# A hybrid S5 and dilated-attention block: the undilated group's values of all head pairs projected in one wide granule beside the scan and taken through DRAM, with attention gates in their place

## The chip, the cores and the metric

The kernel runs on one core of one Trainium2 chip. The metric is the time of one execution on the device in microseconds; several runs are taken and their median is compared. TensorE (PE) does matrix products and transposes into eight PSUM banks of 128 x 512 float32. VectorE (DVE), ScalarE (ACT) and GpSimd (POOL) work on tiles in SBUF and PSUM. SyncE (SP) issues most of the transfers between DRAM and SBUF. Each engine takes its instructions in the order of the program and waits at semaphores for the others.

## The reference

One decoder layer on 512 tokens of width 1024, with a state-space branch and an attention branch that share one projection. Reduced to what matters:

```python
h = rms_norm(x, norm_w)
proj = h @ w_in
u_s, z_s, q, k, v, z_a, r_s, r_a = split(proj)   # 1024, 1024, 1536, 1536, 1536, 512, 1024, 1024 columns
y_s = s5_branch(u_s, ...)                  # diagonal complex scan, GELU, GLU
y_s = (y_s * silu(z_s)) @ w_ssm_out
q, k = rope(rms_norm(q)), rope(rms_norm(k))
y_a = dilated_attention(q, k, v)           # 3 groups of 8 heads of 64; (window, dilation) (128, 1), (512, 4), (2048, 16)
y_a = (y_a * silu(z_a)) @ w_attn_out
m = sigmoid(r_s) * y_s + sigmoid(r_a) * y_a
out = x + m @ w_o
```

The values v of the first group (window 128, dilation 1: the undilated one) and the gates z_a of the attention branch are the two parts of `proj` that the change concerns. Each is 512 columns wide, that is four pairs of heads of 128 columns.

## The kernel before

All products are float32 in three passes: each operand is split in a high part and a rest, and hi·hi, hi·lo and lo·hi are added in PSUM (`mm3`, L133). The weights come from DRAM in pieces of 512 KB in the order of a list, `plan` (L138), two pieces ahead (`look`). For each piece SP issues the load of `w_raw`, ACT makes `w_hi` (L246) and DVE the rest, `w_lo` (L248). `w_raw` has two buffers, `w_hi` and `w_lo` three each.

There are two forms of projection. A unit (`cm_unit`, L251) takes 128 columns of weights as the stationary operand and leaves the result with columns on partitions and tokens along the free axis: 8 x 3 matmuls of 512 into one bank. A wide granule (`wide_granule`, L666) takes 512 columns of weights as the moving operand and leaves four tiles of 128 tokens x 512 columns in four banks: its weights come in four quarters (`kq`), and for each quarter it goes over the four token tiles (`r`) with 6 matmuls each, 96 in all. Both forms need the same matmuls for the same columns. Time in the program is counted in beats: 6 matmuls each, so that a unit has 4 beats and a granule 16.

PSUM tiles are dealt in turn by `ps_tile`:

```python
deal = {"p": [0, 1, 2], "g": [3, 4, 5, 6, 7]}
dealt[kind] += 1
... tag="b%d" % tags[dealt[kind] % len(tags)]
```

The projections use kind p; everything else uses kind g. While a granule runs beside the scan, p has the banks 0 to 3 and g the banks 4 to 7, and the same counter goes on. A tile that gets a bank has to wait for the reader of that bank's last tile.

The projections beside the scan go through the list `order` (L161): after the units of u come four units of attention gates (`za`), eight of state-space gates (`zs`), one unit of undilated values (`v0`), a granule with q, k and v of the first head pair (`v`), and eight units of merge gates (`rs`). Between their beats stand the scan's own steps, by a list of `events` (L944 to L959) with a beat each; DVE does the scan (L744 to L769) while PE projects. The gates go through `silu2` (L613): a tanh on ACT into `th` (L616) and a scalar_tensor_tensor on DVE that reads `th` and the PSUM tile (L617), into `sza` for `za` or into a tile `z` for `zs`, which SP writes to DRAM (`gd`, L627).

The undilated values leave their unit with columns on partitions, and the attention needs them with tokens on partitions, in blocks of 128 consecutive tokens (the tokens of the activations are ordered in four tiles, each with every fourth token). So `v0_unit` (L683) copies the unit's bank to SBUF in permuted order on ACT (`vt`, L686), and a later step `finish` turns it with four transposes on PE (`vtp`) and copies it to `V[:, 0]` on ACT (L692). This is done once beside the scan, for head pair 0, and once in each of the first three rounds of the attention stage, for the next head pair. There `scoring` (L1314) puts `finish` right behind the transposes of q and k (`qtp`, `turn`), which read `qraw`, a tile that DVE makes with the norm and the rope (`qk_norm`, L975 to L998). `skip_bank` (L1300) passes over one bank of kind g where no `finish` stands. All PE instructions are held in the order of the code (`follow`, L62); for the other engines the scheduler decides.

Of the kernel before, what the change touches and what calls it, by code (L numbers as in the profile page):

```python
# [11 lines left out]
F32 = mybir.dt.float32  # L12
# [8 lines left out]
P = 128  # L21
D = 1024
S = 512
KT = D // P
NB = S // P
# [8 lines left out]
NP = 4  # L34
NG = 3
U0, ZS0, Q0, K0, V0, ZA0, RS0, RA0 = 0, 1024, 2048, 3584, 5120, 6656, 7168, 8192
# [16 lines left out]
def tile_hybrid_block(ctx: ExitStack, tc: tile.TileContext, x, positions, norm_w, w_in, lam_re, lam_im,  # L53
# [3 lines left out]
    act, dve, pool, sp = nc.scalar, nc.vector, nc.gpsimd, nc.sync  # L57
# [25 lines left out]
    dram = ctx.enter_context(tc.tile_pool(name="dram", bufs=1, space=DRAM))  # L83
    psum = ctx.enter_context(tc.tile_pool(name="psum", bufs=1, space=PSUM))
    deal = {"p": [0, 1, 2], "g": [3, 4, 5, 6, 7]}
# [22 lines left out]
    def bank(name):  # L108
        return ps_tile("g", name)
# [4 lines left out]
    def t2k(name, dtype=F32):  # L114
        return tmp.tile([P, 512], dtype, name=name, tag="t2k")
# [22 lines left out]
    plan, loaded, look = [], [], 2  # L138
# [11 lines left out]
    def cm_spec(w, c0, kts=KT):  # L150
        return (section(w, 0, kts, (c0, P)), kts, P)

    def wide_spec(w, *cols):
        return [(section(w, 2 * h, 2 * h + 2, *cols), 2, 512) for h in range(4)]
# [3 lines left out]
    def head(base, g, hp):  # L158
        return (base + g * 512 + hp * P, P)

    order = [("za", c) for c in range(NP)] + [("zs", c) for c in range(KT)] + [("v0", 0), ("v", 0)]  # L161
    order += [("rs", c) for c in range(KT)]
    for kind, c in order:
        if kind == "v":
            plan += wide_spec(w_in, head(Q0, 2, 0), head(K0, 2, 0), head(V0, 1, 0), head(V0, 2, 0))
        else:
            plan.append(cm_spec(w_in, {"za": ZA0, "zs": ZS0, "rs": RS0, "ra": RA0, "v0": V0}[kind] + c * P))
    for c in range(KT):
        plan.append(cm_spec(w_glu, c * P))
    for c in range(KT):  # L170
# [1 line left out]
    for hp in range(NP):  # L172
        plan += wide_spec(w_in, head(Q0, 0, hp), head(K0, 0, hp), head(Q0, 1, hp), head(K0, 1, hp))
        if hp == 0:
            plan += [cm_spec(w_in, RA0 + c * P) for c in range(n_ra + 1)]
        else:
            plan += wide_spec(w_in, head(Q0, 2, hp), head(K0, 2, hp), head(V0, 1, hp), head(V0, 2, hp))
            plan.append(cm_spec(w_in, V0 + hp * P))
    for c in range(n_ra + 1, KT):
        plan.append(cm_spec(w_in, RA0 + c * P))  # L180
    for c in range(KT // 2):
# [69 lines left out]
    def cm_unit(rh, rl, kts=KT, ps=None, at=()):  # L251
        hi, lo = get_w()
        if ps is None:
            ps = pj_tile()
        for k in range(kts):
            if k % 2 == 0:
                call(at, k // 2)
            mm3(ps, hi[:, k], lo[:, k], rh[:, k], rl[:, k], k == 0, k == kts - 1)
        return ps


    ident = cst.tile([P, P], F32, name="ident")
# [12 lines left out]
    hT_hi = cst.tile([P, KT, S], F32R, name="hT_hi")  # L275
    hT_lo = cst.tile([P, KT, S], F32R, name="hT_lo")
# [172 lines left out]
    W0, K0B, V0B, Y0 = 16, 49, 74, 88  # L449
# [169 lines left out]
    def za_unit(c, at=()):  # L619
        ps = cm_unit(hT_hi, hT_lo, at=at)  # L620
        silu2(sza[:, c], ps)
# [44 lines left out]
    def wide_granule(th, tl, at=(), halved=False):  # L666

        pss = [pj_tile() for _ in range(NB)] + ([bank("pj")] if halved else [])
        for kq in range(4):
            hi, lo = get_w()  # L670
            for r in range(NB):
                call(at, 4 * kq + r)
                parts = [(pss[r], slice(0, 512))]
                if halved and r == NB - 1:
                    parts = [(pss[r], slice(0, 256)), (pss[NB], slice(256, 512))]
                for ps, c in parts:
                    for k in range(2):
                        kk = 2 * kq + k
                        mm3(ps[:, c], th[:, kk, r * P:(r + 1) * P], tl[:, kk, r * P:(r + 1) * P], hi[:, k, c], lo[:, k, c],
                            kk == 0, kk == KT - 1)  # L680
        return pss

    def v0_unit(hp, V, at=()):  # L683
        ps = cm_unit(hT_hi, hT_lo, at=at)
        vt = t2k("vt")
        act.copy(vt.rearrange("p (b r j) -> p r b j", r=4, b=4), ps.rearrange("p (r b j) -> p r b j", r=4, b=4))  # L686

        def finish():
            pt = bank("vtp")
            for b in range(NB):  # L690
                pe.transpose(pt[:, b * P:(b + 1) * P], vt[:, b * P:(b + 1) * P], ident)
            act.copy(V[:, 0].rearrange("p b c -> p (b c)"), pt)  # L692
        return finish

    qd = dram.tile([2, P, 512], F32, name="qd")

    def qv_granule(V, at=()):
        few = dict(deal)
        deal.update(p=[0, 1, 2, 3], g=[4, 5, 6, 7])
        pss = wide_granule(hT_hi, hT_lo, at)  # L700
        deal.update(few)
        for b in range(2):
            qs = t2k("qs")
            for i in range(2):
                r = 2 * b + i
                act.copy(qs[:, 256 * i:256 * i + 256], pss[r][:, 0:256])
                act.copy(V[:, 1:3, r], pss[r][:, 256:512].rearrange("p (g c) -> p g c", g=2))
            sp.dma_start(qd[b], qs)
# [70 lines left out]
    scan_work += [lambda i=i: step(Xs[:, :, :, i], Xs[:, :, :, i - 1], Xs[:, :, :, i]) for i in range(1, NI)]  # L779

    V = new_v()
    fin = []

    def filler(kind, c, at):
        if kind == "v0":
            fin.append(v0_unit(0, V, at))
        elif kind == "v":
            qv_granule(V, at)
        else:
            {"u": u_unit, "za": za_unit, "zs": zs_unit, "rs": rs_unit}[kind](c, at=at)  # L790
# [103 lines left out]
    def load_us(j):  # L894
        Us[j] = load_u(j, uss[:, 512 * (j % 2):512 * (j % 2) + 512])
# [48 lines left out]
    events = [(3, begin_x), (6, lambda: early.update({3: load_u(3, sza[:, 3])})), (5, f_turn)]  # L944
# [9 lines left out]
    events += [(Y0 + (11 * j + 1) // 3 + 2, lambda j=j: turn_next(j)) for j in range(1, 4)]  # L954
    events += [(W0 + 16, tables_last)]
    events += [(W0 + 26 + 4 * i, lambda i=i: scanning(i, 11)) for i in range(11)]
    events += [(V0B, lambda: fin.pop()()), (Y0 - 10, lambda: load_us(0)), (Y0 - 10, lambda: load_us(1))]
    events += [(Y0 + (11 * j + 1) // 3, lambda j=j: chunk(j)) for j in range(8)] + [(Y0 + 28, lambda: gelu(7, y_turn(7), *gTs))]
    events = sorted(enumerate(events), key=lambda e: (e[1][0], e[0]))  # L959
    events = [e for _, e in events]  # L960
    b0 = 0
    for kind, c in [("u", j) for j in range(3, 8)] + order:
        n = 16 if kind == "v" else 4
        filler(kind, c, [(b - b0, f) for b, f in events if b0 <= b < b0 + n])
        b0 += n
    for b, f in events:
# [58 lines left out]
    def qk_first(at=()):  # L1025

        pss = wide_granule(hT_hi, hT_lo, at)
        raws = [new_raw(0), new_raw(1)]
        sq = sml.tile([P, NB, 8], F32, name="ssq")
        for r in range(NB):  # L1030
            for i in range(2):
                act.copy(raws[i][:, r], pss[r][:, 256 * i:256 * i + 256])
            squares(sq[:, r], pss[r])
        qk_norm((0, 1), raws, sq)
        return raws
# [271 lines left out]
    def turn(hp, g, a):  # L1307
        return lambda: qk_turn(g, (raws[0], raws[1], raw)[g], *QK, turned=(a,))
# [2 lines left out]
        ra_unit(c)  # L1311
    ra_unit(n_ra, [(3, turn(0, 0, 0)), (3, turn(0, 0, 1))])

    def scoring(hp, n, fin):  # L1314
        return [(n, turn(hp, 2, 0)), (n, turn(hp, 2, 1)), (n, fin),
                (n + 3, lambda: dilated(hp, (0, 1), *QK)), (n + 4, lambda: dilated(hp, (2, 3), *QK)),
                (n + 7, lambda: local(hp, *QK)), (n + 7, lambda: settle(hp))]

    def scoring_first(n):
        return [(0, turn(0, 1, 0)), (0, turn(0, 1, 1)), (n, lambda: local(0, *QK)), (n + 2, turn(0, 2, 0)),  # L1320
                (n + 2, turn(0, 2, 1)), (n + 2, skip_bank), (n + 6, lambda: dilated(0, (0, 1), *QK)),
                (n + 7, lambda: dilated(0, (2, 3), *QK)), (n + 7, lambda: settle(0))]

    def turning(hp, n):
        return [(n + i, lambda kind=kind, bb=bb: p_turn(hp, kind, bb))
                for i, (kind, bb) in enumerate(((0, 0), (0, 1), (1, 0), (1, 1)))]

    rals = {}
    fin = skip_bank
    for hp in range(NP):  # L1330
        if hp < NP - 1:
            raws = qk_first(scoring(hp, 3, fin) if hp else scoring_first(4))
            n = 3
            at = turning(hp, n) + [(n + 5, lambda hp=hp: values(hp))]
            at += [(n + 5 + 2 * g + a + (g + a > 0), turn(hp + 1, g, a)) for g in range(2) for a in range(2)]
            raw, Vs[hp + 1] = qk_second(at)
            fin = v0_unit(hp + 1, Vs[hp + 1])
        else:
            for c in range(2):
                rals[c] = gate_tile()  # L1340
                sp.dma_start(rals[c], rad[c])
            at = scoring(hp, 3, fin) + turning(hp, 16)
            for i, c in enumerate(range(n_ra + 1, KT)):
                ra_unit(c, [(n - 4 * i, f) for n, f in at if 4 * i <= n < 4 * i + 4])
            values(hp)
# [64 lines left out]
```

## Time and profile before

| | us |
|---|---|
| median of 3 runs | 672.55 |
| lowest, highest run | 670.82, 672.61 |
| the profiled execution, as timed | 670.11 |
| its span in the trace | 668.0 |
| granted TensorE clock | 1.00 |
| PE busy | 662.0 |
| DVE busy | 464.0 |
| ACT busy | 323.4 |
| POOL busy | 118.1 |

The profiled execution is one of its own, 2.4 us below the median of the runs. Its span goes from the first to the last instruction in the trace, 2.1 us less than its time. Durations in the trace are of single instructions; those on PE overlap with the next one, so the spacing of starts tells what a matmul costs.

### The profile page before, as it was taken

The numbers are of one execution on the slowest core, as the hardware profiler recorded it, in microseconds if no ns is written. First come the engines' busy times: TensorE is split into PE (matmuls) and PEld (weight loads), VectorE is DVE, ScalarE is ACT, GpSimd is POOL, SyncE is SP. The second block draws the span as 40 slices with busy tenths as digits, with TensorE's granted clock in tenths as the row PEclk, the third lists the DMA queues.
The fourth block names the chain that finished last, engine by engine and source line by source line (L and its number), as shares of the span: only waits on it lengthen the run. The fifth ranks groups of instructions, "written<-read, shape, count | busy, mean of one in ns | idle before, by whom it ended". The sixth has DMA issues, their size and how long they took to land.

```text
span 668.0 us, 12363 instructions
## 1 busy us (share of the span) xinstructions
PE 662.0 (99%) x4633; PEld 556.3 (83%) x4633; DVE 464.0 (69%) x965; ACT 323.4 (48%) x680; POOL 118.1 (18%) x274
## 2 busy tenths in 40 slices
PE   8999999999999999999999999999999999999997
PEld 8988888888888888888888888888888888888886
DVE  7999989999786476743238676758575956657531
ACT  6645454422677563422444574557356645633210
POOL 1110000600465258700000030012001200210000
PEclk9999999999999999999999999999999999999999
DMA  9656434743666653563244323222232313347231
GB/s 308 130 137 179 121 95 133 180 142 95 178 141 155 155 169 112 165 216 107 64 126 143 96 64 97 71 74 77 64 94 64 96 35 95 103 147 269 94 127 63
DMA packets 137954, 83.15 MB, mean 124 GB/s; under 512 B 32800, under 2 KB 125992, under 8 KB 137768
## 3 DMA queue, kind: packets, MB, share of 16 engines
q1 hardware_dynamic: 135544, 79.36, 40.2%
q0 software_dynamic: 2048, 2.36, 2.5%
q8 instruction: 36, 0.59, 0.4%
q10 hardware_dynamic: 304, 0.66, 0.3%
q14 instruction: 22, 0.18, 0.1%
HBM read 68.99 MB, written 11.01 MB: 120 GB/s over the span
## 4 chain that ended last, share of the span: by engine, by line
PE 96%; DVE 2%; DMA 1%; ACT 0%; issue 0%; ACTq 0%
PE pj L69 81%; PE sps L69 3%; PE yps L69 3%; PE ot L69 2%; PE ptp L74 2%; PE qtp L74 2%; PE xps L69 1%; PE wps L74 1%; DMA x_all<-in_x_dram 1%; PE kps L69 1%; PE yT L74 1%; DVE w_lo L248 0%; ACT w_hi L246 0%; DVE hT_lo L351 0%; PE vtp L74 0%
## 5 line engine op out<-in xcount | busy, mean ns | idle before, releaser
L246 ACT ACTIVATE w_hi<-w_raw 128x1024 fp32r<-128x1024 f32 x94 | 99.4, 1059 | 164.8 <-PE pj L69 124.8
L248 DVE TENSOR_TENSOR w_lo<-w_raw,w_hi 128x1024 fp32r<-128x1024 f32 x94 | 119.0, 1268 | 62.9 <-ACT w_hi L246 60.7
L69 PE MATMUL pj<-hT_hi,w_hi 128*128 128x512 f32 (+1 forms) x344 | 131.4, 384 | 0.0
L69 PE MATMUL pj<-hT_lo,w_hi 128*128 128x512 f32 (+1 forms) x344 | 128.8, 376 | 0.4 <-DVE hT_lo L351 0.4
L69 PE MATMUL pj<-hT_hi,w_lo 128*128 128x512 f32 (+1 forms) x344 | 126.8, 375 | 0.0
L69 PE MATMUL pj<-w_hi,hT_hi 128*128 128x512 f32 x256 | 102.7, 401 | 0.0
L69 PE MATMUL pj<-w_hi,hT_lo 128*128 128x512 f32 x256 | 99.9, 390 | 0.0
L69 PE MATMUL pj<-w_lo,hT_hi 128*128 128x512 f32 x256 | 99.9, 390 | 0.0
L69 PEld LDWEIGHTS pj<-hT_hi,w_hi 128*128 128x128 f32 x344 | 65.1, 189 | 11.0
L69 PEld LDWEIGHTS pj<-hT_lo,w_hi 128*128 128x128 f32 x344 | 64.9, 189 | 11.1 <-DVE hT_lo L351 0.6
L69 PEld LDWEIGHTS pj<-hT_hi,w_lo 128*128 128x128 f32 x344 | 63.7, 188 | 11.9
L69 PEld LDWEIGHTS pj<-w_hi,hT_lo 128*128 128x128 f32 x256 | 48.1, 188 | 10.4
L69 PEld LDWEIGHTS pj<-w_hi,hT_hi 128*128 128x128 f32 x256 | 48.1, 188 | 9.2
L69 PEld LDWEIGHTS pj<-w_lo,hT_hi 128*128 128x128 f32 x256 | 48.2, 188 | 8.7
L1114 POOL COPY sw<-st 32x4 f32<-32x4 f32 x64 | 11.8, 185 | 172.9 <-ACT Pt L1070 170.1
L1015 DVE SCALAR_TENSOR_TENSOR qkp<-qtp,wcol,qkp 128x512 fp32r<-128x512 f32 (+1 forms) x32 | 23.5, 748 | 25.3 <-ACT qkp L1014 25.2
L1070 ACT ACTIVATE Pt<-Pt,st 128x256 f32<-128x256 f32 (+1 forms) x64 | 30.9, 484 | 19.9 <-DVE st L1068 19.9
L1014 ACT ACTIVATE qkp<-qtp,wcol 128x512 fp32r<-128x512 f32 (+1 forms) x32 | 21.2, 683 | 34.3 <-PE qtp L74 30.9
L840 POOL DMA_DIRECT2D dd<-kt x64 | 33.7, 535 | 2.4 <-POOL kt L836 2.1
L69 PE MATMUL pj<-w_lo,mT_hi 128*128 128x512 f32 (+1 forms) x72 | 26.3, 366 | 0.0
L69 PE MATMUL pj<-w_hi,mT_hi 128*128 128x512 f32 (+1 forms) x72 | 26.3, 366 | 0.0
L69 PE MATMUL pj<-w_hi,mT_lo 128*128 128x512 f32 (+1 forms) x72 | 26.3, 365 | 0.0
(301 smaller groups left out, 1179.8 us busy)
## 6 DMA issues: line engine op xcount, KB each, us to landing
w_raw<-in_w_in_dram SPq DMA_DIRECT2D x36, 512.0 KB
w_raw<-in_w_in_dram SPq DMA_DIRECT2D x128, 128.0 KB
w_raw<-in_w_glu_dram SPq DMA_DIRECT2D x8, 512.0 KB
w_raw<-in_w_ssm_out_dram SPq DMA_DIRECT2D x8, 512.0 KB
w_raw<-in_w_o_dram SPq DMA_DIRECT2D x8, 512.0 KB
w_early<-in_w_in_dram SPq DMA_DIRECT2D x4, 512.0 KB
ud<-uT SPq DMA_DIRECT2D x8, 256.0 KB
uss<-ud SPq DMA_DIRECT2D x8, 256.0 KB
```

The costliest lines, as they stand in the source:

```text
L69: last[0] = nc.tensor.matmul(*a, **k)
L74: last[0] = nc.tensor.transpose(*a, **k)
L246: last_act[0] = act.activation(hi, raw, AF.Copy).ins
L248: dve.tensor_tensor(lo, raw, hi.bitcast(F32), op=ALU.subtract)
L840: pool.dma_start(M[Q * t:Q * t + Q, :, 0:P - Q * t], kt[:, :, t:].rearrange("q g k p -> q g (k p)"))
L1014: act.activation(hi, ps[sl], AF.Copy, scale=w)
L1015: dve.scalar_tensor_tensor(lo, ps[sl], w, hi.bitcast(F32), op0=ALU.mult, op1=ALU.subtract)
L1070: act.activation(o, o, AF.Exp, bias=nm, scale=-1.0, accum_out=st[:, kind, 1, h, b:b + 1])
L1114: pool.tensor_copy(sw[32 * r:32 * r + 32, :, :, b], st[32 * b:32 * b + 32, 1, :, :, r])
```

## The change

`order` has one unit of `za` instead of four, and in place of the unit `v0` a wide granule over the 512 columns of undilated values of all four head pairs. Each of its four token tiles is copied by ACT to an SBUF tile and written by SP to DRAM (`vd`). For each head pair `v0_load` reads its 128 columns back in four transfers, in the order of tokens that the attention needs; for pair 0 ten beats after `V0B`, for the others behind the projection of the round before. In the attention stage each `v0_unit` becomes a `za_unit`, and `skip_bank` takes the place of `finish`. The transposes `vtp` and their copies are gone. Banks for the new granule are set as for the old one, by the same lines, now a function `beside_scan`.

```diff
--- before.py
+++ after.py
@@ -158,13 +158,15 @@
     def head(base, g, hp):
         return (base + g * 512 + hp * P, P)
 
-    order = [("za", c) for c in range(NP)] + [("zs", c) for c in range(KT)] + [("v0", 0), ("v", 0)]
+    order = [("za", 0)] + [("zs", c) for c in range(KT)] + [("v0", 0), ("v", 0)]
     order += [("rs", c) for c in range(KT)]
     for kind, c in order:
-        if kind == "v":
+        if kind == "v0":
+            plan += wide_spec(w_in, (V0, 512))
+        elif kind == "v":
             plan += wide_spec(w_in, head(Q0, 2, 0), head(K0, 2, 0), head(V0, 1, 0), head(V0, 2, 0))
         else:
-            plan.append(cm_spec(w_in, {"za": ZA0, "zs": ZS0, "rs": RS0, "ra": RA0, "v0": V0}[kind] + c * P))
+            plan.append(cm_spec(w_in, {"za": ZA0, "zs": ZS0, "rs": RS0}[kind] + c * P))
     for c in range(KT):
         plan.append(cm_spec(w_glu, c * P))
     for c in range(KT):
@@ -175,7 +177,7 @@
             plan += [cm_spec(w_in, RA0 + c * P) for c in range(n_ra + 1)]
         else:
             plan += wide_spec(w_in, head(Q0, 2, hp), head(K0, 2, hp), head(V0, 1, hp), head(V0, 2, hp))
-            plan.append(cm_spec(w_in, V0 + hp * P))
+            plan.append(cm_spec(w_in, ZA0 + hp * P))
     for c in range(n_ra + 1, KT):
         plan.append(cm_spec(w_in, RA0 + c * P))
     for c in range(KT // 2):
@@ -680,25 +682,30 @@
                             kk == 0, kk == KT - 1)
         return pss
 
-    def v0_unit(hp, V, at=()):
-        ps = cm_unit(hT_hi, hT_lo, at=at)
-        vt = t2k("vt")
-        act.copy(vt.rearrange("p (b r j) -> p r b j", r=4, b=4), ps.rearrange("p (r b j) -> p r b j", r=4, b=4))
-
-        def finish():
-            pt = bank("vtp")
-            for b in range(NB):
-                pe.transpose(pt[:, b * P:(b + 1) * P], vt[:, b * P:(b + 1) * P], ident)
-            act.copy(V[:, 0].rearrange("p b c -> p (b c)"), pt)
-        return finish
-
-    qd = dram.tile([2, P, 512], F32, name="qd")
-
-    def qv_granule(V, at=()):
+    vd = dram.tile([NB, P, 512], F32, name="vd")
+
+    def beside_scan(at):
         few = dict(deal)
         deal.update(p=[0, 1, 2, 3], g=[4, 5, 6, 7])
         pss = wide_granule(hT_hi, hT_lo, at)
         deal.update(few)
+        return pss
+
+    def v0_granule(at=()):
+        pss = beside_scan(at)
+        for r in range(NB):
+            vt = t2k("vt")
+            act.copy(vt, pss[r])
+            sp.dma_start(vd[r], vt)
+
+    def v0_load(hp, V):
+        for r in range(NB):
+            sp.dma_start(V[32 * r:32 * r + 32, 0], vd[r, :, hp * P:hp * P + P].rearrange("(b j) c -> j b c", b=NB))
+
+    qd = dram.tile([2, P, 512], F32, name="qd")
+
+    def qv_granule(V, at=()):
+        pss = beside_scan(at)
         for b in range(2):
             qs = t2k("qs")
             for i in range(2):
@@ -779,11 +786,10 @@
     scan_work += [lambda i=i: step(Xs[:, :, :, i], Xs[:, :, :, i - 1], Xs[:, :, :, i]) for i in range(1, NI)]
 
     V = new_v()
-    fin = []
 
     def filler(kind, c, at):
         if kind == "v0":
-            fin.append(v0_unit(0, V, at))
+            v0_granule(at)
         elif kind == "v":
             qv_granule(V, at)
         else:
@@ -954,13 +960,13 @@
     events += [(Y0 + (11 * j + 1) // 3 + 2, lambda j=j: turn_next(j)) for j in range(1, 4)]
     events += [(W0 + 16, tables_last)]
     events += [(W0 + 26 + 4 * i, lambda i=i: scanning(i, 11)) for i in range(11)]
-    events += [(V0B, lambda: fin.pop()()), (Y0 - 10, lambda: load_us(0)), (Y0 - 10, lambda: load_us(1))]
+    events += [(V0B + 10, lambda: v0_load(0, V)), (Y0 - 10, lambda: load_us(0)), (Y0 - 10, lambda: load_us(1))]
     events += [(Y0 + (11 * j + 1) // 3, lambda j=j: chunk(j)) for j in range(8)] + [(Y0 + 28, lambda: gelu(7, y_turn(7), *gTs))]
     events = sorted(enumerate(events), key=lambda e: (e[1][0], e[0]))
     events = [e for _, e in events]
     b0 = 0
     for kind, c in [("u", j) for j in range(3, 8)] + order:
-        n = 16 if kind == "v" else 4
+        n = 16 if kind in ("v0", "v") else 4
         filler(kind, c, [(b - b0, f) for b, f in events if b0 <= b < b0 + n])
         b0 += n
     for b, f in events:
@@ -1311,8 +1317,8 @@
         ra_unit(c)
     ra_unit(n_ra, [(3, turn(0, 0, 0)), (3, turn(0, 0, 1))])
 
-    def scoring(hp, n, fin):
-        return [(n, turn(hp, 2, 0)), (n, turn(hp, 2, 1)), (n, fin),
+    def scoring(hp, n):
+        return [(n, turn(hp, 2, 0)), (n, turn(hp, 2, 1)), (n, skip_bank),
                 (n + 3, lambda: dilated(hp, (0, 1), *QK)), (n + 4, lambda: dilated(hp, (2, 3), *QK)),
                 (n + 7, lambda: local(hp, *QK)), (n + 7, lambda: settle(hp))]
 
@@ -1326,20 +1332,20 @@
                 for i, (kind, bb) in enumerate(((0, 0), (0, 1), (1, 0), (1, 1)))]
 
     rals = {}
-    fin = skip_bank
     for hp in range(NP):
         if hp < NP - 1:
-            raws = qk_first(scoring(hp, 3, fin) if hp else scoring_first(4))
+            raws = qk_first(scoring(hp, 3) if hp else scoring_first(4))
             n = 3
             at = turning(hp, n) + [(n + 5, lambda hp=hp: values(hp))]
             at += [(n + 5 + 2 * g + a + (g + a > 0), turn(hp + 1, g, a)) for g in range(2) for a in range(2)]
             raw, Vs[hp + 1] = qk_second(at)
-            fin = v0_unit(hp + 1, Vs[hp + 1])
+            v0_load(hp + 1, Vs[hp + 1])
+            za_unit(hp + 1)
         else:
             for c in range(2):
                 rals[c] = gate_tile()
                 sp.dma_start(rals[c], rad[c])
-            at = scoring(hp, 3, fin) + turning(hp, 16)
+            at = scoring(hp, 3) + turning(hp, 16)
             for i, c in enumerate(range(n_ra + 1, KT)):
                 ra_unit(c, [(n - 4 * i, f) for n, f in at if 4 * i <= n < 4 * i + 4])
             values(hp)
```

What this does to the order of instructions is shown at three places, with the names' numbers telling tiles apart. Line numbers are those of each kernel; the changed one is 2 lines further on around L617, 7 in the scan's steps and 6 in the attention stage.

The first place is on PE, beside the scan, at the end of the fourteenth unit of the loop over `order` and the units of u: before, the next is another unit (its `DVE_49` is the reader of a bank three units back). "waits" names the semaphore that the instruction waits for.

```order
L69 MATMUL pj_1526<-hT_hi_87,w_lo_1354 128x512
L69 MATMUL pj_1526<-hT_hi_87,w_hi_1353 128x512
L69 MATMUL pj_1526<-hT_lo_88,w_hi_1353 128x512
L69 MATMUL pj_1526<-hT_hi_87,w_lo_1354 128x512
L69 MATMUL pj_1568<-hT_hi_87,w_hi_1395 128x512 [waits DVE_49]
L69 MATMUL pj_1568<-hT_lo_88,w_hi_1395 128x512
L69 MATMUL pj_1568<-hT_hi_87,w_lo_1396 128x512
L69 MATMUL pj_1568<-hT_hi_87,w_hi_1395 128x512
```

After the change the fourteenth unit is the last of `zs`, and the next instruction is the first of the new granule:

```order
L69 MATMUL pj_1533<-hT_hi_87,w_lo_1361 128x512
L69 MATMUL pj_1533<-hT_hi_87,w_hi_1360 128x512
L69 MATMUL pj_1533<-hT_lo_88,w_hi_1360 128x512
L69 MATMUL pj_1533<-hT_hi_87,w_lo_1361 128x512
L69 MATMUL pj_1569<-w_hi_1402,hT_hi_87 128x512 [waits DVE_49]
L69 MATMUL pj_1569<-w_lo_1403,hT_hi_87 128x512
L69 MATMUL pj_1569<-w_hi_1402,hT_lo_88 128x512
L69 MATMUL pj_1569<-w_hi_1402,hT_hi_87 128x512
```

The tile `pj_1569` is the eighteenth of kind p and is dealt from four banks, `pj_1533` the seventeenth and dealt from three; both get bank 2. The wait on `DVE_49` is now for the reader of `pj_1533`.

The second place is on DVE at the same place of the program, first before the change:

```order
L749 TENSOR_TENSOR scn_522<-scn_522 128x512
L744 TENSOR_TENSOR scn_522<-scn_522 128x1024
L748 TENSOR_TENSOR scn_522<-Xs_548,scn_522 128x512
L248 TENSOR_TENSOR w_lo_1565<-w_raw_1562,w_hi_1564 128x1024
L749 TENSOR_TENSOR scn_522<-scn_522 128x512
L769 MEMSET Xs_548 128x64
L617 SCALAR_TENSOR_TENSOR z_1557<-th_1558,pj_1526 128x512
```

The same rows after the change, where the last one reads the bank that the granule waits for:

```order
L756 TENSOR_TENSOR scn_523<-scn_523 128x512
L751 TENSOR_TENSOR scn_523<-scn_523 128x1024
L755 TENSOR_TENSOR scn_523<-Xs_549,scn_523 128x512
L250 TENSOR_TENSOR w_lo_1576<-w_raw_1573,w_hi_1575 128x1024
L756 TENSOR_TENSOR scn_523<-scn_523 128x512
L776 MEMSET Xs_549 128x64
L619 SCALAR_TENSOR_TENSOR z_1564<-th_1565,pj_1533 128x512
```

Nothing moved here but names and line numbers: the reader of the unit's bank, the last row, stands behind two scan steps, a split of weights and a clearing of `Xs`.

The third place is on DVE in the attention stage, where the first of the three units changes its kind; before:

```order
L987 TENSOR_TENSOR qraw_4651<-qraw_4651,qrstd_4675 128x1024
L248 TENSOR_TENSOR w_lo_4743<-w_raw_4737,w_hi_4742 128x1024
L993 TENSOR_TENSOR rt1_4691<-qraw_4651,tC_3040 128x256
L994 TENSOR_TENSOR rt2_4692<-qraw_4651,tS_3041 128x16x8
L996 TENSOR_TENSOR rt2_4692<-qraw_4651,tS_3041 128x16x8
L998 TENSOR_TENSOR qraw_4651<-rt1_4691,rt2_4692 128x16x16
L1015 SCALAR_TENSOR_TENSOR qkp_3683<-qtp_4764,wcol_84,qkp_3682 128x512
```

After the change:

```order
L250 TENSOR_TENSOR w_lo_4748<-w_raw_4742,w_hi_4747 128x1024
L999 TENSOR_TENSOR rt1_4691<-qraw_4651,tC_3040 128x256
L1000 TENSOR_TENSOR rt2_4692<-qraw_4651,tS_3041 128x16x8
L1002 TENSOR_TENSOR rt2_4692<-qraw_4651,tS_3041 128x16x8
L619 SCALAR_TENSOR_TENSOR sza_337<-th_4735,pj_4710 128x512
L1004 TENSOR_TENSOR qraw_4651<-rt1_4691,rt2_4692 128x16x16
L1021 SCALAR_TENSOR_TENSOR qkp_3683<-qtp_4769,wcol_84,qkp_3682 128x512
```

The new row of `sza` stands between the three products of the rope and their sum, `qraw`.

## The prediction, on record before the run

> **What bounds the kernel now.** I begin with the share of each engine and the chain of work that ended last, since together they say whose time a saving has to come out of.
>
> ```profile
> span 668.0 us, 12363 instructions
> ...
> PE 662.0 (99%) x4633; PEld 556.3 (83%) x4633; DVE 464.0 (69%) x965; ACT 323.4 (48%) x680; POOL 118.1 (18%) x274
> ...
> PE 96%; DVE 2%; DMA 1%; ACT 0%; issue 0%; ACTq 0%
> ```
>
> TensorE is busy for 99% of the span and is 96% of the chain. So a matmul or transpose that goes shortens the span by its own time, and every new moment in which PE waits lengthens it by that moment. Work on other engines counts only where PE waits for it. VectorE is 69% busy on average, but the change acts beside the scan, so I read that stage by itself: the windows view (PE, PEld, DVE, ACT, POOL busy, clock, DMA share, GB/s).
>
> ```profile
> 120.00:130.00 10.00, 10.00 (x45) 8.26 (x44) 9.83 (x15) 3.09 (x4) 8.45 (x16) 1.00 0.74 152
> 140.00:150.00 10.00, 10.00 (x46) 8.24 (x45) 9.83 (x14) 3.08 (x4) 0.00 (x0) 1.00 0.51 158
> ```
>
> VectorE is at 9.83 of 10 us there: whatever is put into its queue comes out late. PE has no gap, because each projection unit fills a PSUM bank that was emptied long before. Which unit waits for which eviction is the question of this change.
>
> **What is removed.** Sixteen transposes on PE, and eight copies of 128x512 on ACT; the projection matmuls stay as many (one wide granule of 96 in place of four units of 24). The groups view (busy us and mean ns of one), then the chain at one place beside the scan and at one in the attention stage (start, us):
>
> ```profile
> L74 PE MATMUL vtp<-ident,vt 128*128 128x128 f32 x16 | 2.4, 272 | 0.0
> L692 ACT COPY V<-vtp 128x512 f32<-128x512 f32 x4 | 2.3, 574 | 1.9 <-PE vtp L74 1.9
> L686 ACT COPY vt<-pj 128x512 f32<-128x512 f32 x4 | 2.3, 563 | 0.0
> L616 ACT ACTIVATE th<-pj 128x512 f32<-128x512 f32 x12 | 6.9, 578 | 0.0
> ```
>
> ```profile
> 150.11 0.44 PE vtp L74 x4
> ```
>
> ```profile
> 435.25 0.44 PE vtp L74 x4
> ...
> 439.49 0.77 DVE qkp L1015
> 440.26 0.04 issue
> 440.30 1.21 PE sps L69 x8
> ```
>
> Each group of four takes 0.44 us of the chain, and there are four groups (one for each pair of heads): **-1.8 us**. The 2.4 us of the group's busy time count overlapping matmuls twice, so the chain's number is used. The ACT copies (four granule copies of 0.56 replace the four unit copies; the four of V, 0.57 each, go; tanh stays at twelve) are worth nothing either way: ACT is at 3.1 of 10 us. The stall before sps at 440.30 stays, as its chain starts when PE ends the first quarter of a granule, which moves with PE.
>
> **The wait that is added.** Banks for projections are dealt in turn: three while units run, four while a granule runs. In the order of dealing, the new granule's first tile is number 18, and 18 mod 4 = 2; the unit just before it is number 17, and 17 mod 3 = 2. It is **the same bank**. So the granule's first matmul has to wait until that last unit's silu has been read out: tanh on ACT and then a scalar_tensor_tensor on DVE (the order's rows show PE's wait on DVE there, and the DVE row that releases it reads pj_1533, the unit just ended). Before, a unit waited for the reader of the unit three earlier, and the old granule's first bank had a whole unit in between. All that PE has queued is behind this matmul, since its matmuls go in program order.
>
> How late that DVE instruction is can be read at the same place of the program before: fourteen units after the start of this loop, where the order has the same instructions on ACT and DVE up to it. The timeline, PE first, then ACT, then DVE:
>
> ```profile
> 125.02 0.39 PE L69 MATMUL pj<-hT_lo,w_hi 128*128 128x512 f32 x1
> 125.24 0.39 PE L69 MATMUL pj<-hT_hi,w_lo 128*128 128x512 f32 x1
> 125.47 0.39 PE L69 MATMUL pj<-hT_hi,w_hi 128*128 128x512 f32 x1
> ```
>
> ```profile
> 125.44 1.07 ACT L246 ACTIVATE w_hi<-w_raw 128x1024 fp32r<-128x1024 f32 x1 [3.90 <-PE pj L69]
> 126.41 0.58 ACT L616 ACTIVATE th<-pj 128x512 f32<-128x512 f32 x1
> ```
>
> ```profile
> 126.04 0.69 DVE L748 TENSOR_TENSOR scn<-Xs,scn 128x512 f32<-128x512 f32 x1
> 126.65 1.22 DVE L248 TENSOR_TENSOR w_lo<-w_raw,w_hi 128x1024 fp32r<-128x1024 f32 x1
> 127.79 0.68 DVE L749 TENSOR_TENSOR scn<-scn 128x512 f32<-128x512 f32 x1
> 128.46 0.65 DVE L617 SCALAR_TENSOR_TENSOR z<-th,pj 128x512 f32<-128x512 f32 x1
> ```
>
> The unit's last matmul starts at 125.24 and the next unit's first at 125.47. ACT first makes the high part of the next weights (w_hi), then the tanh, until 126.99. DVE has a scan step, the weights' low part and another step ahead of the silu, which runs from 128.46 to 129.11. With 0.04 us from DVE's end to PE's start, as before sps above, PE would begin at 129.15 and not at 125.47: **+3.7 us**. Bounds: if DVE took the silu the moment the tanh ended, 126.99 + 0.65 + 0.04 = 127.68, or +2.2 us. If DVE were as late as it was for an earlier gate,
>
> ```profile
> 78.65 0.58 ACT L616 ACTIVATE th<-pj 128x512 f32<-128x512 f32 x1
> ...
> 82.32 0.68 DVE L617 SCALAR_TENSOR_TENSOR sza<-th,pj 128x512 f32<-128x512 f32 x1
> ```
>
> which ended 3.77 us after its tanh (83.00 - 79.23), it would be 130.80, or +5.3. I take 3.7, the row at the same place. Nothing later gives it back: PE has no other wait for DVE in this stage that an earlier DVE would shorten. The granule's other banks were read before, or a unit earlier; its own banks are freed by ACT 0.56 us after each tile's last matmul, four tiles one after another, and the following granule needs them in the same turn.
>
> **The attention stage.** Three units of V become three gate units. The tanh takes the place of the copy on ACT, but the silu is new on DVE, and the order puts it between the third rope product and the sum that makes qraw, which PE's next transposes (qtp) need. The timeline at the three places:
>
> ```profile
> 432.92 0.28 DVE L996 TENSOR_TENSOR rt<-qraw,tS 128x128 f32<-128x128 f32 x1
> ...
> 433.24 0.42 DVE L998 TENSOR_TENSOR qraw<-rt,rt 128x256 f32<-128x256 f32 x1
> ...
> 433.98 1.03 PEld L74 LDWEIGHTS qtp<-ident,qraw 128*128 128x128 f32 x8
> 434.21 1.04 PE L74 MATMUL qtp<-ident,qraw 128*128 128x128 f32 x8
> ```
>
> ```profile
> 497.42 0.42 DVE L998 TENSOR_TENSOR qraw<-rt,rt 128x256 f32<-128x256 f32 x1
> 498.16 0.81 PEld L74 LDWEIGHTS qtp<-ident,qraw 128*128 128x128 f32 x6
> ```
>
> ```profile
> 561.61 0.42 DVE L998 TENSOR_TENSOR qraw<-rt,rt 128x256 f32<-128x256 f32 x1
> 562.35 0.92 PEld L74 LDWEIGHTS qtp<-ident,qraw 128*128 128x128 f32 x7
> ```
>
> qraw is ready at 433.66, and PE loads it at 433.98: 0.32 us to spare; 0.32 at each of the other two (497.84 to 498.16, 562.03 to 562.35). The silu takes 0.65 us (at 128.46), and DVE starts an instruction some 0.08 before the last one's end (126.65 + 1.22 against 127.79), so it holds the queue for about 0.58. Then qraw comes 0.26 us after PE wants it: three times that is +0.8, and 0 if the later weight load can still hide behind the running matmul, which ends at 434.21 for the next start. I take the upper end less a little, **+0.7**.
>
> **The transfers.** The copies of V go out and come back through DRAM on SP's queue: four writes and four reads of each pair's columns, in a stage where a pair of heads takes 64.2 us (qraw's sums at 433.24 and 497.42 above). V is free once the last pair's values are done and is read with the next pair's values, most of those 64 us later. Nothing is charged. SP's order also moves four loads of the scan's input (Uj) behind two weight loads and the C loads:
>
> ```profile
> 77.74 1.10 SPq L799 DMA_DIRECT2D cn<-in_c_re_dram  x2
> ...
> 86.43 0.74 PE L69 MATMUL xps<-Uj,W 128*64 128x64 f32 x18
> ```
>
> They would be issued from 78.8 to about 80 and are first used at 86.43: over 6 us for 256 KB each, in a stage that moves over 100 GB/s. Zero, with up to +3 if the queue ahead of them is late.
>
> **The sum.** 668.0 - 1.8 + 3.7 + 0.7 = 670.6 us of span, +2.6. The profiled execution took 670.11 us, 2.1 more than its span, so it would become 672.7. The runs shown have their median at 672.55, 2.4 above that execution, and the same difference gives **675.2 us**, +0.4%. Differences under 0.3% (2.0 us) are about what a measurement of this kernel cannot tell from no change; the forecast is just over it.
>
> **Rivals.** (1) The wait at the granule's start is short or is not there: DVE reaches the silu at once, or the bank was free. This decides when DVE is less than a scan step behind. At +2.2 the net is +1.1 (673.7); with no wait and none at qraw it is -1.8 (670.8). Against it: DVE at 9.83 of 10 us, and three instructions ahead of the silu in program order. For it: the order says what waits for what, and not when. Not slower; 0.15. (2) The clock falls in the new idle time. PE starts slow in this kernel:
>
> ```profile
> 2.00:3.70 1.70, 1.70 (x10) 1.00 0.81 239
> 5.40:7.10 1.70, 1.70 (x17) 1.00 1.17 378
> ```
>
> The same transposes go at 10 in 1.7 us at first and 17 later (the clock column says 1.00 in both rows, so it has to be read from the counts), so PE comes up to speed only after the first 3.7 us of its work (1.56 to about 5.25). If 3.7 us without work put it back, the next 3.7 us would pass with half the work done: +1.9, in all 677.1; twice that, 679, if the slow stretch is twice as long. Against: the same rows of before show no drop, but there is no idle of this length to show one. Chance 0.15. The Trainium skill, page "TensorE: Matmul & The Clock Gate", section "Part 1: The HAM clock gate (the "warmup" mystery)", says that the clock halves after an idle window of about 3.4 us, in windows that run freely and do not start with the idle time. The slow start agrees; no run here shows a fall in mid-kernel. By the page an idle time hardly longer than the window rarely covers a whole one, so the rule would leave the clock up more often than not. (3) A transfer is late (Uj on SP, or V): +1 to +3 over the sum, 676 to 678; 0.07. (4) The change of form, 128x512 weights in long rows in place of columns, lets PE issue closer: nothing in before shows it, since units and granules both go at 0.23 us per matmul; 0.03, at about 670.
>
> **How the numbers follow.** The forecast has 0.60, with 674.2 to 676.2 as its own range by the attention term and the 0.5 us by which the silu can shift. Range: 672.0 to 678.0; it reaches down into the short wait and up to the clock case. Slower by over 0.3% (above 674.6): three quarters of the forecast's case, the clock, the late transfer: 0.45 + 0.15 + 0.06 = 0.66. Within 0.3%: the rest of the forecast's case and nearly all of the first rival, 0.29. Faster: 0.05, the last rival and the low end of the first.
>
> **What would show it.** In the changed kernel PE has a gap of 3.5 to 4 us at about 125.5, released by DVE's silu of the gates (L619); the matmuls after it stand at 0.23 us apart if the clock holds, 0.45 if not. At the three qtp places a gap of 0.2 to 0.3 us, released by qraw's sum (L1004). No vtp rows. The prediction is wrong if the gap is missing or much shorter, if the kernel waits at xps for Uj, or if V's loads end after the first use of V.

## The result, and the profile after

The changed kernel takes 674.99 us (median of 6 runs, 674.67 to 676.64). The kernel before, with three more runs beside it, takes 671.31 us (6 runs, 670.27 to 672.61). The ratio is 1.0053, with a 95% interval of 1.0043 to 1.0063: slower, by 3.7 us. The profiled execution took 674.70 us with a span of 672.7, against 670.11 and 668.0 before. One run of the kernel fill34 below took 827.64 us at a mean clock of 0.754 in place of 1.00, and it is left out of all that follows.

From the page of the changed kernel, its head, the row of the granted clock by slices (40 slices of 16.8 us each), and the chain by engine:

```profile
span 672.7 us, 12365 instructions
...
PE 663.3 (99%) x4617; PEld 556.0 (83%) x4617; DVE 464.0 (69%) x965; ACT 321.7 (48%) x676; POOL 116.8 (17%) x274
...
PEclk9999999899999999999999999999999999999999
...
PE 94%; DVE 3%; issue 1%; DMA 1%; ACT 0%; DVEq 0%; ACTq 0%
```

PE has less to do (16 transposes are gone) and is nevertheless busy 1.3 us longer. The chain has 94% of PE in place of 96%, and 1% more of DVE and of issue, and the eighth slice, 117.7 to 134.5 us, shows a clock below full. Both point to the new granule's start. PE's timeline there (start, us, what; in brackets the idle time ahead of it and what ended it):

```profile
125.37 0.39 PE L69 MATMUL pj<-hT_hi,w_lo 128*128 128x512 f32 x1
129.31 0.62 PE L69 MATMUL pj<-w_hi,hT_hi 128*128 128x512 f32 x1 [3.55 <-DVE z L619]
129.73 0.63 PE L69 MATMUL pj<-w_lo,hT_hi 128*128 128x512 f32 x1
...
132.29 0.63 PE L69 MATMUL pj<-w_lo,hT_hi 128*128 128x512 f32 x1
132.72 0.51 PE L69 MATMUL pj<-w_hi,hT_lo 128*128 128x512 f32 x1
133.06 0.40 PE L69 MATMUL pj<-w_hi,hT_hi 128*128 128x512 f32 x1
133.29 0.39 PE L69 MATMUL pj<-w_lo,hT_hi 128*128 128x512 f32 x1
```

There are two losses and not one. First PE waits for DVE's silu: without the wait the granule would start at 125.60 (125.37 + 0.23), so the wait costs 3.71 us. Then nine matmuls go slowly, eight of them 0.43 us apart instead of 0.23 and the ninth 0.34, and take 3.75 us (129.31 to 133.06) in place of 2.04 (9 x 0.227): 1.71 us more. The windows view says the same in its column of the clock (after the engine's busy time and count):

```profile
125.00:130.00 5.00, 1.45 (x6) 0.95 0.92 222
130.00:135.00 5.00, 5.00 (x17) 0.70 0.41 126
135.00:140.00 5.00, 5.00 (x24) 1.00 0.00 0
```

The readers' side, ACT and then DVE, is where it was in the kernel before, 0.12 to 0.15 us later, about the two kernels' difference ahead of this place (0.15 at kps in the table below):

```profile
125.57 1.06 ACT L248 ACTIVATE w_hi<-w_raw 128x1024 fp32r<-128x1024 f32 x1 [3.89 <-PE pj L69]
126.53 0.58 ACT L618 ACTIVATE th<-pj 128x512 f32<-128x512 f32 x1
```

```profile
126.80 1.22 DVE L250 TENSOR_TENSOR w_lo<-w_raw,w_hi 128x1024 fp32r<-128x1024 f32 x1
127.94 0.68 DVE L756 TENSOR_TENSOR scn<-scn 128x512 f32<-128x512 f32 x1
128.61 0.65 DVE L619 SCALAR_TENSOR_TENSOR z<-th,pj 128x512 f32<-128x512 f32 x1
```

Starts of the same PE instruction in both traces show where the time goes (after less before, worked out from the timelines; kps and yps are tiles of the scan stage, ot is the product with V in the attention stage):

| up to | before, us | after, us | difference |
|---|---|---|---|
| kps, ahead of the granule | 114.65 | 114.80 | +0.15 |
| first yps, behind both granules | 169.57 | 174.65 | +5.08 |
| first ot of the attention stage | 408.41 | 413.45 | +5.04 |
| last ot | 595.30 | 599.75 | +4.45 |
| last product | 664.41 | 668.85 | +4.44 |

The scan stage costs +4.93: 3.71 + 1.71 less 0.44 for its four transposes, with 0.05 to spare. The attention stage gives back 0.59. From the last product's start to the end of the span it is 3.59 us before and 3.85 after; this 0.26 makes the 4.7 us of the span, and its cause is open.

At the three qtp places the silu stands ahead of the sum, as the order said, and PE waits for qraw. The first of them, DVE and then PE (PEld is its load of weights):

```profile
438.27 0.69 DVE L619 SCALAR_TENSOR_TENSOR sza<-th,pj 128x512 f32<-128x512 f32 x1
438.88 0.42 DVE L1004 TENSOR_TENSOR qraw<-rt,rt 128x256 f32<-128x256 f32 x1
...
439.35 0.14 PEld L74 LDWEIGHTS qtp<-ident,qraw 128*128 128x128 f32 x1 [0.37 <-DVE qraw L1004]
439.35 0.33 PE L74 MATMUL qtp<-ident,qraw 128*128 128x128 f32 x1
```

Moved on by the 5.04 us of that stretch, qtp would start at 439.25 (434.21 + 5.04). It starts at 439.35: 0.10 us late, and 0.11 at the other two. Neither the loads of V nor those of Uj appear among PE's waits.

### The profile page after: what moved, and what is told of

Same layout as the page of the kernel before. It is cut to its first block, busy times and chain, and to the rows that moved or that the text cites. A ratio compares the mean times of both kernels' runs of the same rounds, so it can differ in the third digit from the quotient of the medians.

```text
span 672.7 us, 12365 instructions
## 1 busy us (share of the span) xinstructions
PE 663.3 (99%) x4617; PEld 556.0 (83%) x4617; DVE 464.0 (69%) x965; ACT 321.7 (48%) x676; POOL 116.8 (17%) x274
## 4 chain that ended last, share of the span: by engine, by line
PE 94%; DVE 3%; issue 1%; DMA 1%; ACT 0%; DVEq 0%; ACTq 0%
PE pj L69 79%; PE sps L69 3%; PE yps L69 3%; PE ot L69 2%; PE ptp L74 2%; PE qtp L74 2%; PE xps L69 1%; PE wps L74 1%; DMA x_all<-in_x_dram 1%; PE yT L74 1%; DVE scn L751 1%; PE kps L69 1%; DVE scn L756 1%; DVE scn L755 0%; DVE w_lo L250 0%
## 5 line engine op out<-in xcount | busy, mean ns | idle before, releaser
L69 PE MATMUL pj<-w_hi,hT_hi 128*128 128x512 f32 x288 | 115.9, 402 | 3.6 <-DVE z L619 3.6
L69 PE MATMUL pj<-hT_hi,w_hi 128*128 128x512 f32 (+1 forms) x312 | 119.1, 384 | 0.0
L69 PE MATMUL pj<-hT_lo,w_hi 128*128 128x512 f32 (+1 forms) x312 | 116.3, 375 | 0.4 <-DVE hT_lo L353 0.4
L69 PE MATMUL pj<-hT_hi,w_lo 128*128 128x512 f32 (+1 forms) x312 | 114.4, 374 | 0.0
L69 PE MATMUL pj<-w_lo,hT_hi 128*128 128x512 f32 x288 | 113.0, 393 | 0.0
L69 PE MATMUL pj<-w_hi,hT_lo 128*128 128x512 f32 x288 | 113.0, 392 | 0.0
L69 PEld LDWEIGHTS pj<-hT_lo,w_hi 128*128 128x128 f32 x312 | 58.8, 189 | 9.9 <-DVE hT_lo L353 0.6
L69 PEld LDWEIGHTS pj<-w_hi,hT_hi 128*128 128x128 f32 x288 | 54.5, 189 | 14.6 <-DVE z L619 4.0
L69 PEld LDWEIGHTS pj<-w_hi,hT_lo 128*128 128x128 f32 x288 | 54.5, 189 | 11.9
L69 PEld LDWEIGHTS pj<-w_lo,hT_hi 128*128 128x128 f32 x288 | 54.5, 189 | 10.1
```

The lines of the kernel that those rows point to most:

```text
L69: last[0] = nc.tensor.matmul(*a, **k)
```

## The experiments

Two questions are open: is the wait really that of the bank, and how late its reader is; and does the clock fall because of the idle time, and from what length of it? All kernels below are the changed kernel with one edit, the last one with two. Their ratios are to runs of the kernel before taken beside each, whose medians went from 670.57 to 671.57 us.

**Moving the bank within the granule.** One, two or three banks are passed over before the granule, so that the last gate's bank comes as its fourth, third or second tile:

```diff
     def v0_granule(at=()):
+        dealt["p"] += 1
         pss = beside_scan(at)
```

(2 and 3 in place of 1 in the other two.)

> One bank of kind p is passed over before the new granule, so that its four tiles get the banks 3, 0, 1, 2 and the bank of the last gate unit comes last, 4.1 us after the granule's start. Theory (the new wait is for that bank, and the clock falls only because of the wait): PE has no gap at 125.6, the clock stays at 1.00, and 3.7 us of wait and 1.7 us of slow matmuls go: span about 667.3, 0.7 us under the kernel before. Rival (DVE is late at this place whatever the bank, so PE waits for the next weights or the scan instead): the gap only moves by a microsecond or two and the span stays above 670.

> Two banks are passed over: the last gate unit's bank is the granule's third tile, 2.72 us after its start. Theory: the silu still ends at 129.3, so PE waits about 1.0 us before the third tile (129.3 - 125.6 - 2.7); the clock holds, as an idle time of 1 us has not lowered it anywhere in the kernel before; span about 668.3. If the gap does not follow the place of the bank, the theory of the bank falls.

> Three banks are passed over: the last gate unit's bank is the granule's second tile, 1.36 us after its start. Theory: a wait of about 2.35 us before the second tile. If the clock falls only after some 3.4 us of idle time it holds here: span about 669.7. If 2.3 us are enough for it to fall, a row of matmuls at 0.43 us follows and the span is about 671.4.

PE's timeline at the granule's start with one bank passed over:

```profile
125.35 0.39 PE L69 MATMUL pj<-hT_hi,w_lo 128*128 128x512 f32 x1
125.57 0.39 PE L69 MATMUL pj<-w_hi,hT_hi 128*128 128x512 f32 x1
```

With two, at the third tile:

```profile
128.19 0.39 PE L69 MATMUL pj<-w_hi,hT_lo 128*128 128x512 f32 x1
129.40 0.50 PE L69 MATMUL pj<-w_hi,hT_hi 128*128 128x512 f32 x1 [0.82 <-DVE z L619]
```

And with three, at the second tile:

```profile
126.71 0.39 PE L69 MATMUL pj<-w_hi,hT_lo 128*128 128x512 f32 x1
129.29 0.50 PE L69 MATMUL pj<-w_hi,hT_hi 128*128 128x512 f32 x1 [2.19 <-DVE z L619]
129.63 0.40 PE L69 MATMUL pj<-w_lo,hT_hi 128*128 128x512 f32 x1
129.86 0.40 PE L69 MATMUL pj<-w_hi,hT_lo 128*128 128x512 f32 x1
```

The end of the wait stays at 129.3 to 129.4, and its start moves with the bank, by 1.36 us a tile. With the bank last, no wait is left. The waits (start to start, less the usual 0.23) are 0, 0.98 and 2.35 us, against 0, 1.0 and 2.35 expected. The spans are 668.3, 668.5 and 669.8 (expected 667.3, 668.3 and 669.7); the 1.0 us of the first comes from a later place, told at the end, and five of its ten runs have 667.3 to 667.4. The times are 669.44 us (ratio to before 0.9975, 0.9966 to 0.9984), 670.42 (0.9984, 0.9975 to 0.9993) and 673.73 (1.0041, 1.0021 to 1.0061). The 669.44 us of the first are 5.55 us under the changed kernel's median, where the wait and the slow matmuls make 3.71 + 1.71 = 5.42. For the last the expectation left the clock open: the profiled execution holds it, with matmuls at 0.23 us, but four of the six runs have a mean clock of 0.997 and spans of 671.6 to 673.3, and two have 0.999 or more and 669.8 and 669.9. So 2.2 us of idle time can be enough, but are not always.

**Keeping PE at work during the wait.** The banks stay; transposes of the identity, read by nobody, go ahead of the granule into the tile that it fills last:

```diff
         pss = [pj_tile() for _ in range(NB)] + ([bank("pj")] if halved else [])
+        for i in range(fill):
+            pe.transpose(pss[NB - 1][:, 128 * (i % 4):128 * (i % 4) + 128], ident, ident)
```

with `fill` 34 or 20 for the new granule and 0 elsewhere.

> The banks are as in the changed kernel; 34 transposes of the identity matrix, which nothing reads, are put on PE ahead of the granule into its fourth tile, to keep PE at work while it waits. Theory (wait and clock are two prices): the granule's first product still starts at about 129.3, as it waits for the silu, but the products after it stand 0.23 us apart at once, and the span is 1.7 us under the changed kernel's, about 671.0. Rival (the slow products come from something else, such as the change of form or the load of V's weights): they stay slow, and the span stays at 672.7.

> As fill34 with 20 transposes, so that PE's idle time before the granule is about 1.5 us in place of 3.7 (129.3 - 125.6 - 20 x 0.109) and the wait for the silu is the same. The clock fell in all six runs with 3.7 us of idle time, in four of six with 2.2 us (skip3), in none of ten with 0.8 us (skip2). If it falls by the length of the idle time alone, from about 2 us on, it holds in all runs here: products 0.23 us apart, mean clock 1.00, time 672.5 to 673.5. If a shorter idle time can do it when it lies badly in a window that runs by itself, some runs show 0.997 and are 1.7 us longer than the others.

PE's timeline with 34:

```profile
125.60 0.39 PE L69 MATMUL pj<-hT_hi,w_lo 128*128 128x512 f32 x1
125.83 3.87 PE L74 MATMUL pj<-ident 128*128 128x128 f32 x34
129.55 0.50 PE L69 MATMUL pj<-w_hi,hT_hi 128*128 128x512 f32 x1
129.88 0.40 PE L69 MATMUL pj<-w_lo,hT_hi 128*128 128x512 f32 x1
130.12 0.39 PE L69 MATMUL pj<-w_hi,hT_lo 128*128 128x512 f32 x1
```

And with 20:

```profile
125.75 2.35 PE L74 MATMUL pj<-ident 128*128 128x128 f32 x20
129.46 0.50 PE L69 MATMUL pj<-w_hi,hT_hi 128*128 128x512 f32 x1 [1.36 <-DVE z L619]
129.79 0.39 PE L69 MATMUL pj<-w_lo,hT_hi 128*128 128x512 f32 x1
130.03 0.40 PE L69 MATMUL pj<-w_hi,hT_lo 128*128 128x512 f32 x1
```

The granule starts as late as before, so the wait is untouched, but its products stand 0.23 us apart from the second on: without idle time, or with 1.4 us of it, the clock holds, in all five runs of each. At the first yps the traces are 1.59 and 1.58 us ahead of the changed kernel's (173.29 and 173.22 against 174.65, after taking out 0.23 and 0.15 us by which they are later ahead of the granule). That is the price of the clock, seen apart from the wait; the other 0.1 of the 1.71 us is the first product behind the wait, which takes 0.33 us at full clock too. The span and the time did not show it. The profiled executions have spans of 672.3, against 671.0 expected, and 673.2 (a time of 672.5 to 673.5 was expected); the place told at the end took 0.9 us of it with 34 and 1.8 with 20. The times, 674.06 (1.0039, 1.0026 to 1.0052) and 674.27 us (1.0054, 1.004 to 1.0067), are 0.9 and 0.7 us under the changed kernel's, and not 1.7. No run of either kernel has a span near 671.0 (the lowest are 671.7 and 672.2), so that the filling gains the 1.6 us in the whole kernel's time is not shown.

**Another reader of the same bank.** The last unit ahead of the granule becomes a merge gate, which ACT alone reads:

```diff
-    order = [("za", 0)] + [("zs", c) for c in range(KT)] + [("v0", 0), ("v", 0)]
-    order += [("rs", c) for c in range(KT)]
+    order = [("za", 0)] + [("zs", c) for c in range(KT - 1)] + [("rs", 0), ("v0", 0), ("v", 0)]
+    order += [("zs", KT - 1)] + [("rs", c) for c in range(1, KT)]
```

> Banks as in the changed kernel, but the last unit ahead of the new granule is a merge gate (rs), whose bank is read by the tanh on ScalarE alone; the last state-space gate comes behind the two granules instead. Theory (the price of the wait is how late the reader's own queue is): the same bank is waited for, but only until the tanh ends, 126.53 + 0.58 in the changed kernel, so PE starts the granule at about 127.15 and not at 129.31, idle for 1.5 us; the clock holds at that length in every run, as in fill20; span about 668.8. Rival (PE waits for VectorE there whatever reads the bank, because w_lo or the scan is late): the start stays near 129 and the clock falls again in most runs.

ACT and PE in the timeline:

```profile
126.53 0.58 ACT L634 ACTIVATE th<-pj 128x512 f32<-128x512 f32 x1
...
127.16 0.50 PE L69 MATMUL pj<-w_hi,hT_hi 128*128 128x512 f32 x1 [1.41 <-ACT th L634]
```

PE starts at 127.16, within a hundredth of what was expected, and the clock holds in all eleven runs (0.999 or 1.000). DVE is as busy as before (9.78 of 10 us from 120 to 130 us, against 9.83 in the changed kernel), and PE no longer waits for it here. The time is 671.54 us, 1.0001 (0.9989 to 1.0012) of the kernel before: the wait that is left, 1.6 us (127.16 - 125.36 - 0.23), is about what the change gains without a wait (skip1 is 0.25%, or 1.7 us, under the kernel before).

**The silu behind qraw.** On top of the first edit (one bank passed over), the silu of a gate is put behind the last sum of qraw:

```diff
-        dve.scalar_tensor_tensor(dst, th, 1.0, ps, op0=ALU.add, op1=ALU.mult)
+        with queued_after(sum_last[0]):
+            dve.scalar_tensor_tensor(dst, th, 1.0, ps, op0=ALU.add, op1=ALU.mult)
...
-            dve.tensor_tensor(rh[:, :, :, 0:16], t1, t2, op=ALU.add)
+            sum_last[0] = dve.tensor_tensor(rh[:, :, :, 0:16], t1, t2, op=ALU.add).ins
```

> As skip1, and in the attention stage the silu of each gate unit goes behind the sum that makes qraw on VectorE, and not in front of it. Theory (the silu delays qtp by 0.10 us at each of three places): qtp starts 0.10 us earlier against its neighbours in each round and the time falls by 0.3 us, to about 669.1; the gates' bank is read 0.4 us later, which nobody waits for. Rival (the next chain, through the first quarter's end to sps, takes it back): no change against skip1's 669.44.

DVE and PE at the first of the three places:

```profile
434.01 0.42 DVE L1008 TENSOR_TENSOR qraw<-rt,rt 128x256 f32<-128x256 f32 x1
434.47 0.69 DVE L622 SCALAR_TENSOR_TENSOR sza<-th,pj 128x512 f32<-128x512 f32 x1
...
434.99 0.28 PE L74 MATMUL qtp<-ident,qraw 128*128 128x128 f32 x1
```

qraw now ends 0.56 us ahead of qtp, and qtp is 0.10 us nearer to its neighbours in each round. Against the first edit the trace goes from +0.10 us ahead of these places to -0.35 at the last ot, 0.15 a round. The time is 669.13 us, 0.9979 (0.997 to 0.9988) of the kernel before. This is the fastest median of all, though the runs cannot tell it from the first edit alone (0.9975); that it gains rests on the trace.

## Why the prediction came out as it did

The time, 674.99, is close to the 675.2 forecast, and the sign is right. But the sum was made of +2.6 us and the runs show +3.7, the traces +4.7. The number is close by luck: the median of three runs that it was laid on, 672.55, is 1.2 us above the one of six.

- **The wait, +3.7 us: right, in place, cause and size.** 3.71 us, at 125.6, released by the silu of the unit just ended. Moving the bank moved its start by the tile's 1.36 us and left its end; another reader ended it when that reader's queue did.
- **The clock: the step that failed.** It was priced well as a rival (+1.9; 1.71 measured) and given 0.15. It came in all six runs of the changed kernel, whose mean clock is 0.995 or 0.997, where the kernel before has 0.999 or more (53 runs beside the experiments). With PE kept at work through the wait it did not come (fill34, fill20). The reason for the low chance was that before showed no idle time of this length, and, beside it, a rule of the Trainium skill, page "TensorE: Matmul & The Clock Gate", section "Part 1: The HAM clock gate (the "warmup" mystery)": the clock falls after an idle window of some 3.4 us, in windows that run freely. By that an idle time of 3.55 us should seldom hold a whole window, and one of 2.2 never. The runs say otherwise (6 of 6, and 4 of 6), and the measurement decides.
- **The removed transposes, -1.8 us:** 0.44 us beside the scan. In the attention stage a group took only 0.36 (435.08 to 435.44 in the timeline before): the chain's 0.44 holds a slower first product behind the group (0.32 us), and after the change the first product behind qtp is as slow (0.33).
- **The silu in front of qraw, +0.7 us:** 0.10 us a round and not 0.26. qraw ended at 439.30, 0.28 us after the load of it would have started (433.98 + 5.04), so the lateness was read well. But the load and the first transpose now start together, at 439.35, where before the load stood 0.23 us ahead (433.98 and 434.21). So the end "if the later weight load can still hide", which was named as the lower one, was nearly right. The stage as a whole gives 0.59 us, against 1.32 - 0.7 = 0.6 by the sum, and this too is luck: the transposes and the silu by themselves make 3 x (0.36 - 0.10) = 0.8, and the other 0.2 are lost in small steps in the same rounds, whose cause is open.
- **The transfers, 0:** right. Neither Uj nor V is waited for.
- **Not slower, a short wait:** did not come; DVE had just the three rows ahead of the silu that the trace of before has.

So the change as such does pay, a little: with one bank passed over it makes the kernel 0.25% faster (0.16% to 0.34%), where the kernel as changed is 0.5% slower.

## What to carry to other kernels

When units of different width share a round of PSUM banks, look at each change of form for which bank comes first: a bank costs PE nothing only if its last reader is done by the time PE comes to it (here 3.7 us after the unit's end), and the price is how late that reader's queue is, not only how long the reader takes. A wait of two microseconds or more on a PE that is otherwise full can cost more than itself, because what follows may run at half speed (here behind 2.2 us in four runs of six, behind 3.6 in six of six); look at the spacing of the matmuls behind every gap. Where the wait can't be moved, a reader on an idler engine shortens it (here from 3.71 us to 1.57) and may keep the clock up.

## What the runs showed of the hardware

**The clock and the idle time.** By the length of PE's idle time ahead of the granule, from the profile of each kernel, and the runs' mean clock:

| idle, us | kernel | runs with the clock at 0.997 or less |
|---|---|---|
| 0 | skip1 | 0 of 10 |
| 0 | fill34 | 0 of 5 |
| 0.82 | skip2 | 0 of 10 |
| 1.36 | fill20 | 0 of 5 |
| 1.41 | rs_first | 0 of 11 |
| 2.19 | skip3 | 4 of 6 |
| 3.55 | the changed kernel | 6 of 6 |

The shortest idle time behind which the clock can fall lies between 1.4 and 2.2 us in this kernel; behind 2.2 us it fell by chance, behind 3.6 us each time. In the changed kernel's two runs at 0.995 the span is 673.9 and 674.7 us, 1.2 and 2.0 us above the shortest: a second or a longer stretch of half speed would fit, but there is no profile of such a run. What the hardware counts was not tried.

**A microsecond that comes and goes.** Spans of one kernel often differ by about 1 or 2 us (before: 668.1, 669.1 and 670.2 are common). In four profiles (skip1, skip1_late, fill34 and fill20) PE loses 0.9 to 1.8 us at one place, in the GLU stage; whether the other runs lose theirs there is not known. There PE waits for gT_lo, the rest of a product that DVE makes. PE, DVE and POOL of skip1:

```profile
243.91 0.39 PE L69 MATMUL pj<-gT_hi,w_hi 128*128 128x512 f32 x1
245.10 0.50 PE L69 MATMUL pj<-gT_lo,w_hi 128*128 128x512 f32 x1 [0.80 <-DVE gT_lo L123]
```

```profile
243.18 1.27 DVE L505 TENSOR_SCALAR rope<-rope 128x32 f32<-128x32 f32 x1
244.36 0.68 DVE L123 SCALAR_TENSOR_TENSOR gT_lo<-gq,gT_hi 128x512 fp32r<-128x512 f32 x1
```

```profile
242.75 1.65 POOL L1257 TENSOR_TENSOR zl<-zl,gsum 128x512 f32<-128x512 f32 x1 [4.55 <-DMA zl<-gd]
```

And DVE and POOL of the kernel before at the same instructions:

```profile
243.57 0.17 DVE L503 TENSOR_SCALAR rope<-rope 128x32 f32<-128x32 f32 x1
243.66 0.69 DVE L123 SCALAR_TENSOR_TENSOR gT_lo<-gq,gT_hi 128x512 fp32r<-128x512 f32 x1
243.85 1.65 POOL L1250 TENSOR_TENSOR zl<-zl,gsum 128x512 f32<-128x512 f32 x1 [5.25 <-DMA zl<-gd]
```

The same small instruction takes 0.17 us or 1.27, and the long one ends with POOL's product (244.45 and 244.40). In the kernel before, POOL's product begins at 243.85, when that instruction is over. In all nine profiles the small instruction is long (1.25 to 1.27) where POOL's product began first (skip1, fill34, fill20), ends within 0.05 us of it there, and takes 0.17 or 0.18 in the other six. When POOL's product begins depends on when a transfer lands, which differs from profile to profile. The Trainium skill, page "SBUF — State Buffer", section "Who interferes with whom", says that DVE and GpSimd share a pair of ports, and that where both need it the one that issues first holds it for its whole instruction, while the other is blocked. These rows agree, though they do not show which instructions need the pair. In skip1_late the small instruction is short, and PE still waits 0.86 us for gT_lo. There DVE is late from further ahead:

```profile
240.55 0.26 DVE L1226 TENSOR_SCALAR qkw<-qkw 128x192 f32<-128x192 f32 x1 [2.12 <-DMA qkw<-in_q_norm_w_dram]
```

It waited for a small load, and began at 239.35 in skip1, where PE and not the load ended its wait. In fill20 both come together (the small load is waited for until 244.48). So the place has more than one cause, and by these rows each of them goes back to when a transfer lands. None of it was tried by a kernel, and it hides differences under 1 us unless many runs are compared.
